# Griffin-style block with product-key experts on one core: the split of p is taken apart from its product, a gathered block's rows get a second buffer, a selection step ends at GpSimd's part

## The chip, the cores and the metric

One core of a Trainium2 chip runs the whole program. The engines are TensorE (PE, matmuls; PEld is its weight load), VectorE (DVE), ScalarE (ACT), GpSimd (POOL) and SyncE (SP, which here issues loads and stores). Each works through its own list of instructions in order, and semaphores tie the lists together. The metric is device time in microseconds (us), the median of several runs.

## What is computed

One layer of an encoder block for 1024 tokens of width 1024, in float32. Only the last part, the PEER feed-forward, is touched by the change:

```python
def peer_ffn(hn, w_query, sub_keys, expert_u, expert_v):   # per chunk xc of 128 tokens
    q = (xc @ w_query).reshape(c, PEER_HEADS, 2, PEER_HALF_DIM)
    sc = jnp.einsum('chpd,hpnd->chpn', q, sub_keys)          # scores of 2 x 128 keys, 8 heads
    s1, i1 = lax.top_k(sc[:, :, 0], 16)
    s2, i2 = lax.top_k(sc[:, :, 1], 16)
    cand = s1[..., :, None] + s2[..., None, :]               # 256 pairs
    top, pos = lax.top_k(cand.reshape(c, 8, 256), 16)        # 16 experts of 128*128, per head
    g = softmax(top)
    a = gelu(einsum('chkd,cd->chk', expert_u[eidx], xc))
    return einsum('chk,chkd->cd', g * a, expert_v[eidx])
...
h = h + peer_ffn(rmsnorm(h, ffn_norm_w), ...)
return rmsnorm(h, final_norm_w)
```

## The kernel before

The 1024 tokens are eight tiles of 128. First come the projections, attention, convolution, gates, and the query scores of all tiles; none of that is changed. After that the experts are computed, in two ways at once.

**Dense, for five tiles (640 tokens).** All 16384 experts are run over all 640 tokens, 128 experts at a time: 128 rounds, which this text calls expert blocks, numbered `i`. Operands are split into a high part (a rounded copy) and a low part (the difference), and each product takes three matmuls: high by high, high by low, low by high. One round does this:

- `expert_z`: PE multiplies the block's 128 rows of `expert_u` (tiles `uh`, `uhl`) with the tokens (`actTh`, `actTl`) into `z`, 48 matmuls of 320 columns. ACT takes the Gelu of `z` into `pr` (line 942).
- `expert_p`: DVE multiplies `pr` by the weights `wt` (line 946). Then `split` makes two tiles of it: ACT copies it, rounded, into `ph` (line 906), and DVE subtracts `ph` from `pr` into `phl` (line 908). So on DVE two instructions stand next to each other, and the second needs a result of ACT that needs the first.
- `expert_v`: the block's rows of `expert_v` are loaded and split in the same way (`vh` by ACT, `vhl` by DVE), and `expert_u(i + 1)` loads and splits the next round's `uh` and `uhl`.
- `expert_out`: PE multiplies `ph`, `phl` of two finished blocks with `vh`, `vhl`. There are ten pieces (five token tiles, two halves of 512 columns), five in an even round and five in an odd round. Four of the ten stay in PSUM for the whole loop (`held`). The other six are called moving: each goes to one of two PSUM buffers (`pout`), and DVE adds it to `hacc` in SBUF (line 975). A moving piece can start on PE only when DVE has added the piece two before it. The even round has the pieces moving, held, moving, held, moving; the odd round has held, moving, held, moving, moving. The callback `after` is called before the second piece of a round, and does the product and the split of p.

**Gathered, for three tiles (384 tokens), which the names call blocks `c`.** For each of 128 chosen experts per token, POOL issues an indirect load of 128 rows of 2048 floats (`uvt`, line 741, four buffers). DVE forms the dot product with the block's own rows `hng` (line 748), ACT makes the weight (lines 750 and 751), and DVE adds the weighted second half to `acc` (line 761). `hng` has one buffer and is loaded by SP at the start of each of the three blocks (line 737). These steps come from a generator, `gather_gen`.

**Selection of the three gathered tiles.** `select_gen` finds the experts of a tile in two halves, step by step: top 16 on DVE (`top16`), and at the end, for each of two index lists, a comparison on DVE (line 637), a multiplication on POOL (line 639) and a reduction of its result on DVE (line 640). All three stand in one step.

**What sets the order.** PE and DVE run in the order in which the code is written from the dense loop on; ACT, POOL and SP are ordered by the scheduler. The side jobs are interleaved by `tick`: each group of matmuls counts off its nominal time, and a generator's next step is written out whenever its period is used up. A gather step has a period of 2.36 us while the selection runs and 1.78 us after it; a selection step has 13 us (`SEL_STEP_D`). One round counts off 12.8 us.

Of the kernel before, what the change touches and what calls it, by code (L numbers as in the profile page):

```python
# [10 lines left out]
F32 = mybir.dt.float32  # L11
BF16 = mybir.dt.bfloat16
F32R = mybir.dt.float32r
# [7 lines left out]
P = 128  # L21
S = 1024
D = 1024
# [4 lines left out]
GB = NB * P  # L28
# [17 lines left out]
PHB = 4  # L46
# [6 lines left out]
WFB = 2  # L53
GATHER = (2.36, 1.78)
SEL_STEP = 1.5
SEL_STEP_D = 13
W_STEP = 1.6
MIXW = 3
ATT = (5, 4)
# [6 lines left out]
def block_kernel(ctx, tc, x, wqkv, wcols, wpr, wo, wq, skT, uv, uT, an_w, fn_w, fin_w, sub_w,  # L66
                 conv_w, lq1, lk1, lq2, lk2, cosT, sinT, out):
    nc = tc.nc
    V, A, PL, PE, SP = nc.vector, nc.scalar, nc.gpsimd, nc.tensor, nc.sync
# [524 lines left out]
    def select_gen(small, tt, ev, gw, done=None):  # L594
        hh = PH // 2
        sh = [P, hh, TOPK, TOPK]
        s3 = [P, hh, TOPK]

        t = small

        for a in range(2):
            sc = t([P, PH, NK], F32, "sc")
            SP.dma_start(out=sc, in_=sc_d[tt * P:(tt + 1) * P, a * PH * NK:(a + 1) * PH * NK]
                         .rearrange("p (h c) -> p h c", c=NK))
            sv, si = t([P, PH, TOPK], F32, "sv"), t([P, PH, TOPK], U32, "si")
            for hp in range(PH):
                top16(t, sc[:, hp, :], NK, sv[:, hp, :], si[:, hp, :])
                yield
            ohs = sc.rearrange("p h c -> p (h c)").bitcast(BF16).rearrange("p (j h a k) -> p j h a k", j=2, a=TOPK, k=TOPK)
            sf = t([P, PH, TOPK], F32, "sf")  # L610
            V.tensor_copy(out=sf, in_=si)
            svv = sv.rearrange("p (h q) k -> p h q k", q=2)
            sfv = sf.rearrange("p (h q) k -> p h q k", q=2)
            tv, ti = t(s3, F32, "tv"), t(s3, U32, "ti")
            cd = t([P, hh, CAND], F32, "cd")
            for c0, a0, na, nb in ((0, 0, 4, TOPK), (64, 4, TOPK - 4, 4)):
                sc2 = [P, hh, na, nb]
                V.tensor_tensor(out=cd[:, :, c0:c0 + na * nb].rearrange("p h (a b) -> p h a b", b=nb),
                                in0=svv[:, :, 0, a0:a0 + na].unsqueeze(3).broadcast_to(sc2),
                                in1=svv[:, :, 1, :nb].unsqueeze(2).broadcast_to(sc2), op=ALU.add)  # L620
            yield
            for h in range(hh):
                top16(t, cd[:, h, :], CAND, tv[:, h, :], ti[:, h, :])
                yield
            for j in range(2):
                pi, pj, pf = t(s3, U32, "pi"), t(s3, U32, "pj"), t(s3, BF16, "pf")
                if j == 0:
                    V.tensor_scalar(pi, ti, 4, None, op0=ALU.logical_shift_right)
                    V.tensor_scalar(pj, ti, 2, None, op0=ALU.logical_shift_right)
                    V.scalar_tensor_tensor(pf, pj, -12.0, pi, op0=ALU.add, op1=ALU.max)  # L630
                else:
                    V.tensor_scalar(pi, ti, 12, None, op0=ALU.bitwise_and)
                    V.tensor_scalar(pj, ti, 3, None, op0=ALU.bitwise_and)
                    V.scalar_tensor_tensor(pf, ti, 64.0, pi, op0=ALU.is_lt, op1=ALU.mult)
                    V.tensor_tensor(out=pf, in0=pf, in1=pj, op=ALU.add)
                oh = ohs[:, j]
                V.tensor_tensor(out=oh, in0=pf.unsqueeze(2).broadcast_to(sh), in1=iota_k.unsqueeze(1).broadcast_to(sh),
                                op=ALU.is_equal)
                PL.tensor_tensor(out=oh, in0=oh, in1=sfv[:, :, j, :].unsqueeze(3).broadcast_to(sh), op=ALU.mult)
                V.tensor_reduce(out=ev[j][:, a * 64:(a + 1) * 64].rearrange("p (h k) -> p h k", k=TOPK),  # L640
                                in_=oh.rearrange("p h a k -> p h k a"), axis=AX.X, op=ALU.add)
                yield
            dv = t(s3, F32, "dv")
            V.tensor_tensor(out=dv, in0=tv, in1=tv[:, :, 0:1].broadcast_to(s3), op=ALU.subtract)
            A.activation(tv, dv, AF.Exp)
            zz = t([P, hh], F32, "zz")
            V.tensor_reduce(out=zz, in_=tv, axis=AX.X, op=ALU.add)
            V.reciprocal(out=zz, in_=zz)
            V.tensor_tensor(out=gw[:, a * 64:(a + 1) * 64].rearrange("p (h k) -> p h k", k=TOPK), in0=tv,
                            in1=zz.unsqueeze(2).broadcast_to(s3), op=ALU.mult)  # L650
            if done:
                done(a * 64, (a + 1) * 64)
            yield
# [73 lines left out]
    def gather_gen(gat):  # L727
        st = {}

        def slot():  # L730
            return gat.tile([P, 2 * D], F32, name="uvt", tag="uvt", bufs=UVT)

        def fetch(c, k):
            if k == 0:
                st[c] = gat.tile([P, D], F32, name="hng", tag="hng")
                rows = slice(sels[c][0] * P, (sels[c][0] + 1) * P)
                SP.dma_start(out=st[c], in_=hn_d[rows, :])
                st["acc", c] = gat.tile([P, D], F32, name="acc", tag="acc")
                SP.dma_start(out=st["acc", c], in_=h_d[rows, :])
            t = slot()  # L740
            PL.indirect_dma_start(out=t[:], out_offset=None, in_=uv,  # L741
                                  in_offset=bass.IndirectOffsetOnAxis(ap=sels[c][1][:, k:k + 1], axis=0))
            return c, k, t

        def dot(c, k, t):
            u = t[:, 0:D]
            zt = tiny.tile([P, 1], F32, name="zt", tag="zt")
            V.scalar_tensor_tensor(u, u, 1.0, st[c], op0=ALU.mult, op1=ALU.mult, accum_out=zt)  # L748
            wt = tiny.tile([P, 1], F32, name="wt", tag="wt")
            A.activation(wt, zt, AF.Gelu)  # L750
            A.activation(wt, wt, AF.Copy, scale=sels[c][2][:, k:k + 1])
            return c, k, t, wt, fetch_last() if k == NE - 1 else None

        def fetch_last():
            t = slot()
            SP.dma_start(out=t[:, 0:D], in_=bass.AP(tensor=fin_w.tensor, offset=fin_w.offset, ap=[[0, P], [1, D]]))
            return t[:, 0:D], t[:, D:2 * D]

        def accumulate(c, k, t, wt, end):
            acc = st["acc", c]  # L760
            V.scalar_tensor_tensor(acc, t[:, D:2 * D], wt, acc, op0=ALU.mult, op1=ALU.add)  # L761
            yield
            if end:
                fw, y = end
                ss = tiny.tile([P, 1], F32, name="ss_o", tag="ss_o")
                A.activation(y, acc, AF.Square, accum_out=ss)
                if c < NA - 1:
                    yield
                r = rstd_of(ss, D, 1, "o")
                state["normed"] = c  # L770
                yield
                V.scalar_tensor_tensor(y, acc, r, fw, op0=ALU.mult, op1=ALU.mult)
                SP.dma_start(out=out[sels[c][0] * P:(sels[c][0] + 1) * P, :], in_=y)

        held = dotted = None
        for c in range(NA):
            while c >= len(sels):
                yield
            for k in range(NE):
                while k >= got[sels[c][0]]:  # L780
                    yield
                new = fetch(c, k)
                if held:
                    held = dot(*held)
                    yield
                    if dotted:
                        yield from accumulate(*dotted)
                    dotted = held
                held = new
        held = dot(*held)  # L790
        yield
        yield from accumulate(*dotted)
        yield from accumulate(*held)
# [99 lines left out]
    du, dn, dv, hp, gat = (pool(n) for n in ("du", "dn", "dv", "hp", "gat"))  # L893
# [51 lines left out]
    def expert_p(i, p):  # L945
        V.tensor_mul(p.rearrange("p (c t) -> p c t", t=WT), p.rearrange("p (c t) -> p c t", t=WT),
                     wts[i // WB][:, :, i % WB, :])
        return split(p, "ph", PHB, [P, GB], V)

    def expert_v(i):  # L950
        vr = raw_rows(uv[i * P:(i + 1) * P, D:])
# [10 lines left out]
    def expert_out(pv, vv, part, first, last, after):  # L962
        n = len(order) // BLK
        for j, (t, hf) in enumerate(order[part * n:(part + 1) * n]):
            if j == 1:
                after()
            ds = slice(hf * 512, (hf + 1) * 512)
            lhs = [(p[0][:, t * P:(t + 1) * P], p[1][:, t * P:(t + 1) * P]) for p in pv]
# [31 lines left out]
    for i in range(NK + BLK):  # L1000
        b, part = i // BLK - 1, i % BLK
        made = []
# [4 lines left out]
                us.append(expert_u(i + 1))  # L1007

        def product():
            if made:  # L1010
                pv.append(expert_p(i, made.pop()))

        if i < NK:
            made.append(expert_z(i, us.pop(0), ahead))
        if b >= 0:
            expert_out(pv[:BLK], vv[:BLK], part, b == 0, b == NK // BLK - 1, product)
        product()
        if b >= 0 and part == BLK - 1:
            pv, vv = pv[BLK:], vv[BLK:]
        if i < NK:  # L1020
# [70 lines left out]
```

## Time and profile before

| | |
|---|---|
| median of 3 runs | 3399.04 us (3398.12 to 3399.4) |
| profiled execution | 3390.54 us, its span 3388.8 us |
| busy share of the span | PE 91%, PEld 83%, DVE 78%, ACT 38%, POOL 26% |
| mean granted TensorE clock | 0.959 of full speed |
| dense loop in the span | from 1315 us to 3370 us |
| loaded and stored | 801 MB |

A busy share is an average over all stages. In the dense loop two engines are nearly full, so what each of them waits for, and where, says more than the shares. In rows of the trace a name to the left of the arrow is what an instruction writes, to the right what it reads, and the bracket at the end tells how long its engine had stood idle and what ended that.

### The profile page before, as it was taken

How to read it: one execution, taken by the hardware profiler on the slowest of the kernel's cores; microseconds unless marked ns; L12 is line 12 of the kernel's file. 1: busy time of each engine (PE TensorE's matmuls, PEld its weight loads, DVE VectorE, ACT ScalarE, POOL GpSimd, SP SyncE). 2: the span in 40 equal slices, each digit the busy share in tenths (PEclk: the TensorE clock that was granted, in tenths of full speed). 3: DMA queues.
4: the chain of work that ended last, by engine and by line, in shares of the span. 5: the costliest groups of instructions: out<-in, count | busy, mean ns of one | idle time of the engine just before them, and what ended most of it. 6: DMA issues, size and time to landing. Idle time of an engine off the chain costs nothing.

```text
span 3388.8 us, 45651 instructions
## 1 busy us (share of the span) xinstructions
PE 3073.1 (91%) x17551; PEld 2804.0 (83%) x17551; DVE 2659.0 (78%) x4661; ACT 1295.8 (38%) x2341; POOL 889.2 (26%) x712
## 2 busy tenths in 40 slices
PE   8999999898989887998998998998999988999896
PEld 6799988798988787887887887887888877888785
DVE  4442564589999965988898987888988888888888
ACT  3322462446577674323223323323223332333232
POOL 2310000154353542222222222222222322223232
PEclk9999999899999998999999998999999998999999
DMA  4442223735443656777787877787777888898886
GB/s 172 156 152 73 85 87 118 248 127 212 162 176 145 230 217 240 279 268 268 273 291 262 286 267 254 278 285 254 285 282 248 325 308 303 324 324 329 293 323 247
DMA packets 237547, 801.09 MB, mean 236 GB/s; under 512 B 18832, under 2 KB 123280, under 8 KB 174096
## 3 DMA queue, kind: packets, MB, share of 16 engines
q0 software_dynamic: 64704, 442.53, 35.3%
q1 hardware_dynamic: 152592, 305.30, 26.5%
q10 hardware_dynamic: 20032, 50.34, 3.9%
q8 instruction: 138, 2.26, 0.3%
q14 instruction: 81, 0.66, 0.1%
HBM read 714.74 MB, written 83.36 MB: 236 GB/s over the span
## 4 chain that ended last, share of the span: by engine, by line
PE 26%; issue 24%; DVE 22%; DMA 11%; POOL 9%; ACT 7%; SPq 0%; POOLq 0%; ACTq 0%; DVEq 0%
POOL uvt L741 8%; DMA raw<-in_uT 6%; PE pg L228 4%; DVE acc L761 3%; DVE uvt L748 3%; PE pq L228 3%; PE z L915 3%; PE ph L228 2%; DVE hacc L975 2%; PE py L228 2%; DVE vhl L908 2%; PE pout L915 2%; PE pw L694 2%; DVE phl L908 1%; DMA uvt<-in_uv,idx 1%
## 5 line engine op out<-in xcount | busy, mean ns | idle before, releaser
L741 POOL DMA_INDIRECT uvt<-in_uv,idx x384 | 498.4, 1298 | 1498.3 <-DVE acc L761 1447.3
L915 PE MATMUL z<-actTh,uhl 128*128 128x320 f32 x2048 | 645.1, 315 | 13.6 <-DVE uhl L908 13.6
L915 PE MATMUL z<-actTh,uh 128*128 128x320 f32 x2048 | 647.4, 316 | 7.7 <-ACT pr L942 5.8
L915 PE MATMUL z<-actTl,uh 128*128 128x320 f32 x2048 | 645.5, 315 | 0.0
L748 DVE SCALAR_TENSOR_TENSOR uvt<-uvt,hng 128x1024 f32<-128x1024 f32 x384 | 467.5, 1217 | 54.2 <-DMA uvt<-in_uv,idx 26.9
L761 DVE SCALAR_TENSOR_TENSOR acc<-uvt,wt,acc 128x1024 f32<-128x1024 f32 x384 | 490.7, 1278 | 5.3 <-DMA acc<-h_d 5.0
L915 PE MATMUL pout<-vh,ph 128*128 128x512 f32 x768 | 319.0, 415 | 175.9 <-DVE hacc L975 175.8
L915 PEld LDWEIGHTS z<-actTh,uh 128*128 128x128 f32 x2048 | 398.4, 195 | 15.4 <-ACT pr L942 6.7
L915 PEld LDWEIGHTS z<-actTh,uhl 128*128 128x128 f32 x2048 | 396.8, 194 | 14.0 <-DVE uhl L908 14.0
L915 PEld LDWEIGHTS z<-actTl,uh 128*128 128x128 f32 x2048 | 397.6, 194 | 6.6
L750 ACT ACTIVATE wt<-zt 128x1 f32<-128x1 f32 x384 | 77.0, 201 | 721.3 <-DVE uvt L748 721.0
L915 PEld LDWEIGHTS pout<-vh,ph 128*128 128x128 f32 x768 | 149.0, 194 | 231.8 <-DVE hacc L975 204.5
L915 PE MATMUL pout<-vhl,ph 128*128 128x512 f32 x768 | 311.7, 406 | 1.6 <-DVE vhl L908 1.6
L915 PE MATMUL pout<-vh,phl 128*128 128x512 f32 x768 | 311.6, 406 | 0.0
L975 DVE TENSOR_TENSOR hacc<-pout,hacc 128x512 f32<-128x512 f32 x384 | 262.2, 685 | 28.9 <-PE pout L915 27.9
L717 POOL TENSOR_TENSOR o<-ms,wtr 128x512 f32<-128x512 bf16 x160 | 204.5, 1322 | 255.0 <-PE pw L694 132.4
L185 DVE TENSOR_TENSOR wl<-wr,wh 128x2048 fp32r<-128x2048 f32 x66 | 157.9, 2393 | 113.9 <-ACT wh L184 113.9
L906 ACT CAST uh<-raw 128x1024 fp32r<-128x1024 f32 x128 | 134.7, 1052 | 280.1 <-DMA raw<-in_uT 226.0
L908 DVE TENSOR_TENSOR phl<-pr,ph 128x640 fp32r<-128x640 f32 x128 | 105.6, 825 | 152.6 <-ACT ph L906 151.0
L694 PE MATMUL pw<-o,o 128*128 128x128 f32 x1280 | 172.4, 288 | 39.5 <-POOL o L717 19.1
L184 ACT CAST wh<-wr 128x2048 fp32r<-128x2048 f32 x74 | 141.0, 1907 | 164.4 <-DMA wr<-in_wq 33.2
L694 PEld LDWEIGHTS pw<-o,o 128*128 128x128 f32 x1280 | 164.2, 202 | 47.6 <-POOL o L717 24.0
(290 smaller groups left out, 6831.2 us busy)
## 6 DMA issues: line engine op xcount, KB each, us to landing
raw<-in_uT SPq DMA_DIRECT2D x128, 512.0 KB
raw<-in_uv SPq DMA_DIRECT2D x128, 512.0 KB
w_d<-wbuf ACTq DMA_DIRECT2D x20, 2048.0 KB
wt<-w_d SPq DMA_DIRECT2D x32, 1280.0 KB
wr<-in_wcols SPq DMA_DIRECT2D x28, 1024.0 KB
wr<-in_wq SPq DMA_DIRECT2D x24, 1024.0 KB
xt<-in_x SPq DMA_DIRECT2D x16, 512.0 KB
q_d<-qt POOLq DMA_DIRECT2D x32, 256.0 KB
```

What stands on the lines that cost most here:

```text
L184: A.copy(out=op[0][sl], in_=src)
L185: lo.tensor_sub(op[1][sl], src, op[0][sl].bitcast(F32))
L228: PE.matmul(pd, lhsT=l[a], rhs=r[b], start=i == 0 and j == 0, stop=i == n - 1 and j == len(c) - 1)
L694: PE.matmul(pw[:, u, :], lhsT=o2[:, t + u, :], rhs=o1[:, t + u, :], start=True, stop=True)
L717: PL.tensor_tensor(out=o1.rearrange("p t i -> p i t"), in0=ms[:, 0], in1=w[:, ts].unsqueeze(1).broadcast_to(sh), op=ALU.mult)
L741: PL.indirect_dma_start(out=t[:], out_offset=None, in_=uv, in_offset=bass.IndirectOffsetOnAxis(ap=sels[c][1][:, k:k + 1], axis=0))
L748: V.scalar_tensor_tensor(u, u, 1.0, st[c], op0=ALU.mult, op1=ALU.mult, accum_out=zt)
L761: V.scalar_tensor_tensor(acc, t[:, D:2 * D], wt, acc, op0=ALU.mult, op1=ALU.add)
L906: A.copy(out=hi, in_=t)
L908: eng.tensor_sub(lo, t, hi.bitcast(F32))
L915: PE.matmul(ps, lhsT=lhs[k][a], rhs=rhs[k][b], start=first and k == 0 and j == 0, stop=last and k == n - 1 and j == 2)
L975: V.tensor_add(hacc[:, t - NR, ds], ps, hacc[:, t - NR, ds])
```

## The change

There are three edits, all of which act in the dense loop.

1. The split of p. `expert_p` now does the product on DVE and the copy on ACT, and leaves out the subtraction. That is a function of its own, `expert_lo`, which is called at the next call of `after`; and `after` is called before the second and before the fourth piece of a round.
2. `hng` has two buffers.
3. A selection step of a gathered tile ends after POOL's multiplication, so the reduction stands in the following step. Each half then has 18 steps for 16, and the period goes from 13 to 11.6 us: 208.8 us for a half, after 208.

```diff
-SEL_STEP_D = 13
+SEL_STEP_D = 11.6
...
                 PL.tensor_tensor(out=oh, in0=oh, in1=sfv[:, :, j, :].unsqueeze(3).broadcast_to(sh), op=ALU.mult)
+                if done:
+                    yield
                 V.tensor_reduce(out=ev[j][:, a * 64:(a + 1) * 64].rearrange("p (h k) -> p h k", k=TOPK),
...
-                st[c] = gat.tile([P, D], F32, name="hng", tag="hng")
+                st[c] = gat.tile([P, D], F32, name="hng", tag="hng", bufs=2)
...
-        return split(p, "ph", PHB, [P, GB], V)
+        hi = dv.tile([P, GB], F32R, name="ph", tag="ph", bufs=PHB)
+        A.copy(out=hi, in_=p)
+        return p, hi
+
+    def expert_lo(p, hi):
+        lo = dv.tile([P, GB], F32R, name="phl", tag="phl", bufs=PHB)
+        V.tensor_sub(lo, p, hi.bitcast(F32))
+        return hi, lo
...
-            if j == 1:
+            if j in (1, 3):
                 after()
...
         def product():
-            if made:
-                pv.append(expert_p(i, made.pop()))
+            if made and isinstance(made[0], tuple):
+                pv.append(expert_lo(*made.pop()))
+            elif made:
+                made[0] = expert_p(i, made[0])
...
-        product()
+        while made:
+            product()
```

The order of instructions on PE is the same as before, and so are all lists ahead of the dense loop. Three places show what moves. The first is DVE in an odd round of the dense loop: `pr<-pr,wt` is the product, `phl<-pr,ph` the subtraction, `hacc` the three moving pieces, and `uvt,zt` and `acc` are gather steps. Before:

```order
L946 TENSOR_TENSOR pr<-pr,wt 128x640
L908 TENSOR_TENSOR phl<-pr,ph 128x640
L975 TENSOR_TENSOR hacc<-pout,hacc 128x512
L761 SCALAR_TENSOR_TENSOR acc<-uvt,wt,acc 128x1024
L975 TENSOR_TENSOR hacc<-pout,hacc 128x512
```

Now, in such a round:

```order
L948 TENSOR_TENSOR pr<-pr,wt 128x640
L984 TENSOR_TENSOR hacc<-pout,hacc 128x512
L763 SCALAR_TENSOR_TENSOR acc<-uvt,wt,acc 128x1024
L956 TENSOR_TENSOR phl<-pr,ph 128x640
L642 TENSOR_REDUCE e_18983<-sc 128x64
L984 TENSOR_TENSOR hacc<-pout,hacc 128x512
```

One moving piece's addition and one gather step now stand between the product and the subtraction; the reduction of the selection happens to follow here.

The second place is DVE at a selection step of a gathered tile: `sc<-pf,iota_k` is the comparison, and the reduction writes `e`. Before:

```order
L637 TENSOR_TENSOR sc<-pf,iota_k 128x1024
L640 TENSOR_REDUCE e_18969<-sc 128x64
L975 TENSOR_TENSOR hacc<-pout,hacc 128x512
L908 TENSOR_TENSOR vhl<-raw,vh 128x1024
L748 SCALAR_TENSOR_TENSOR uvt,zt<-uvt,hng 128x1024
```

Now:

```order
L637 TENSOR_TENSOR sc<-pf,iota_k 128x1024
L763 SCALAR_TENSOR_TENSOR acc<-uvt,wt,acc 128x1024
L984 TENSOR_TENSOR hacc<-pout,hacc 128x512
L956 TENSOR_TENSOR phl<-pr,ph 128x640
L750 SCALAR_TENSOR_TENSOR uvt,zt<-uvt,hng 128x1024
L984 TENSOR_TENSOR hacc<-pout,hacc 128x512
L910 TENSOR_TENSOR vhl<-raw,vh 128x1024
L763 SCALAR_TENSOR_TENSOR acc<-uvt,wt,acc 128x1024
L910 TENSOR_TENSOR uhl<-raw,uh 128x1024
L750 SCALAR_TENSOR_TENSOR uvt,zt<-uvt,hng 128x1024
L642 TENSOR_REDUCE e_18983<-sc 128x64
```

The reduction stands ten instructions later, and what follows the comparison at once is an addition of the gather, whose operands both lie in SBUF.

The third place is SP's queue at the start of the dense loop. Before, the loads of the first gathered block are followed by the dense loop's:

```order
L737 DMA hng<-hn_d 128x1024
L739 DMA acc<-h_d 128x1024
L934 DMA wt<-w_d 128x20x128
L923 DMA raw<-in_uv 128x1024
L923 DMA raw<-in_uT 128x1024
```

Now:

```order
L739 DMA hng<-hn_d 128x1024
L741 DMA acc<-h_d 128x1024
L936 DMA wt<-w_d 128x20x128
L739 DMA hng<-hn_d 128x1024
L925 DMA raw<-in_uv 128x1024
L925 DMA raw<-in_uT 128x1024
```

The second block's `hng` is loaded here, ahead of two of the dense loop's loads, and no longer at that block's start.

## Rows read from the trace of the kernel before

**Rows 1.** Windows: start:end length, busy per engine, clock, DMA share, GB/s

```profile
1315.00:1366.00 51.00, 33.29 (x175) 31.19 (x176) 21.41 (x33) 14.17 (x24) 8.24 (x7) 0.77 0.88 313
1366.00:2624.00 1258.00, 1158.02 (x6244) 1041.80 (x6243) 1092.13 (x1781) 383.56 (x769) 298.93 (x228) 0.96 0.77 272
2624.00:3336.00 712.00, 637.26 (x3430) 573.43 (x3429) 616.59 (x777) 219.66 (x489) 205.02 (x156) 0.96 0.87 315
```

**Rows 2.** Waits of PE, 1315 to 3370: sum in us, times, longest

```profile
PE pout L915 <- DVE hacc L975: 175.8, 65, 12.1
```

**Rows 3.** Waits of DVE, 1366 to 2624

```profile
DVE phl L908 <- ACT ph L906: 85.3, 79, 3.3
DVE e L640 <- POOL sc L639: 20.7, 10, 2.1
DVE hacc L975 <- PE pout L915: 20.4, 23, 2.7
DVE pr L946 <- ACT pr L942: 17.0, 10, 5.5
```

**Rows 4.** Waits of DVE, 2624 to 3336

```profile
DVE phl L908 <- ACT ph L906: 61.5, 44, 8.2
DVE uvt L748 <- DMA uvt<-in_uv,idx: 19.8, 25, 2.0
DVE hacc L975 <- PE pout L915: 4.8, 5, 2.0
```

**Rows 5.** PE in order of time, 2637 to 2652: start, duration, instruction

```profile
2637.57 0.31 PE L915 MATMUL z<-actTh,uh 128*128 128x320 f32 x1
...
2651.49 0.31 PE L915 MATMUL z<-actTh,uh 128*128 128x320 f32 x1
```

**Rows 6.** PE in order of time around a wait, 2663 to 2669

```profile
2663.82 0.39 PE L915 MATMUL pout<-vh,phl 128*128 128x512 f32 x1
2667.73 0.73 PE L915 MATMUL pout<-vh,ph 128*128 128x512 f32 x1 [3.52 <-DVE hacc L975]
2668.26 0.63 PE L915 MATMUL pout<-vhl,ph 128*128 128x512 f32 x1
```

**Rows 7.** Windows, right behind that wait

```profile
2667.70:2670.30 2.60, 2.57 (x6) 2.11 (x7) 2.60 (x3) 0.95 (x1) 0.95 (x1) 0.53 0.45 186
```

**Rows 8.** DVE in order of time, 1407 to 1412

```profile
1407.49 0.82 DVE L946 TENSOR_TENSOR pr<-pr,wt 128x640 f32<-128x640 f32 x1
1409.11 0.83 DVE L908 TENSOR_TENSOR phl<-pr,ph 128x640 fp32r<-128x640 f32 x1 [0.80 <-ACT ph L906]
1409.85 1.28 DVE L761 SCALAR_TENSOR_TENSOR acc<-uvt,wt,acc 128x1024 f32<-128x1024 f32 x1
1411.05 0.68 DVE L975 TENSOR_TENSOR hacc<-pout,hacc 128x512 f32<-128x512 f32 x1
```

**Rows 9.** ACT in order of time, same place

```profile
1406.84 1.06 ACT L906 CAST uh<-raw 128x1024 fp32r<-128x1024 f32 x1
...
1408.35 0.73 ACT L906 CAST ph<-pr 128x640 fp32r<-128x640 f32 x1
```

**Rows 10.** Waits of DVE, 1315 to 3370

```profile
DVE phl L908 <- ACT ph L906: 151.0, 126, 8.2
DVE uvt L748 <- DMA hng<-hn_d: 26.8, 2, 25.1
```

**Rows 11.** POOL in order of time, 1079.7 to 1081.9

```profile
1079.76 1.94 POOL L639 TENSOR_TENSOR sc<-sc,sf 128x1024 bf16<-128x1024 bf16 x1 [3.64 <-DVE rz L395]
```

**Rows 12.** DVE in order of time, 1079.7 to 1081.9

```profile
1079.59 0.16 DVE L395 RECIPROCAL rz<-zs 128x2 f32<-128x2 f32 x1
1079.79 1.92 DVE L396 SCALAR_TENSOR_TENSOR rz<-rz,nlam,zs 128x1 f32<-128x1 f32 x1
```

**Rows 13.** POOL in order of time, 3067.0 to 3067.3

```profile
3067.26 1.68 POOL L741 DMA_INDIRECT uvt<-in_uv,idx  x1 [2.99 <-DVE acc L761]
```

**Rows 14.** DVE in order of time, 3076.8 to 3077.1

```profile
3077.00 1.23 DVE L748 SCALAR_TENSOR_TENSOR uvt<-uvt,hng 128x1024 f32<-128x1024 f32 x1 [1.23 <-DMA uvt<-in_uv,idx]
```

## The prediction

> **What bounds the kernel now.** The edits act only in the dense loop, so I began with the windows by stage, and took its two long parts: 1258 us with the selection beside the gather (80 rounds) and 712 us without it (44 rounds) [rows 1]. In both, DVE is busy for 87% and PE for 89 to 92%, so the next question is which of them waits for the other. PE's waits have one large row: 175.8 us, 65 times, for DVE's addition to `hacc` [rows 2]; that is one round in two, the odd one, whose last two pieces are both moving. DVE's waits for PE are small: 20.4 and 17.0 us in the first part (the second of these through ACT's Gelu), 4.8 us in the other [rows 3, 4]. So DVE sets the pace, and PE stands when DVE is behind. DVE's largest loss is not work but a wait for ACT: the subtraction `phl` behind the copy `ph`, 85.3 and 61.5 us [rows 3, 4], 151.0 us over the loop [rows 10].
>
> How much could be won at all is read from PE in an undisturbed round: from the first `z` matmul of one to that of the next 13.92 us [rows 5]. The two parts take 1258 / 80 = 15.72 and 712 / 44 = 16.18 us a round. At 13.92 us they would be shorter by 144 and 100 us. A wait of PE costs more than its length: behind one of 3.52 us the granted clock was 0.53 for 2.60 us, the lower of the two levels for nearly all of it, which is about 1.2 us more [rows 6, 7].
>
> **The split of p.** The number of instructions is unchanged: 128 products, copies and subtractions. What changes is what stands between product and subtraction. In the timeline of DVE the product starts at 1407.49 and takes 0.82; ACT's copy runs from 1408.35 for 0.73, and the subtraction starts at 1409.11, after 0.80 us of standing [rows 8, 9]. Now an addition of a moving piece (0.68) and mostly a gather step (1.28 for `acc`) stand there [rows 8], 1.9 us or so, which covers 0.80. That is 0.80 x 126 = 101 us of the 151.0. The other 50 us belong to copies that come late, up to 8.2 us [rows 10]: on ACT the cast `uh` of the next expert block, which waits for a load, stands ahead of `ph` [rows 9], and the new list of ACT still has it there. The cover exceeds 0.80 by about 1.1 us, so of each late copy up to 1.1 us more is hidden; I take 30 of the 50. Together -131 us of DVE time; bounds -101 (no late copy gains) and -151. In the odd round the subtraction moreover stands behind the first addition to `hacc`, which PE is waiting for; that comes 0.80 + 0.74 us earlier.
>
> No new wait is queued behind: the copy needs only gather steps that stand before the product on DVE, as it did. What is held longer is `pr`, which has one buffer; the subtraction is done some 2 us later, while the next Gelu comes only when PE has gone through the next `z`, some half of a round later, so that is at no cost.
>
> **The selection step.** It removes DVE's wait for POOL's multiplication, 20.7 us, 10 times [rows 3]. But the wait has a second cause that stays. Earlier in the program the multiplication ran for 1.94 us from 1079.76, and a DVE instruction of one column, started 0.03 us later, took 1.92 us and ended with it, where its neighbour of two columns took 0.16 [rows 11, 12]. So a DVE instruction that meets the multiplication can be held to its end. In the new order seven of the ten comparisons are followed by a gather step, with both operands in SBUF, the other three by an addition from PSUM and only then by such an instruction. I take -3 us, bounds 0 and -20.7.
>
> The Trainium skill ("SBUF — State Buffer", section "SBUF: two separate sides") says that VectorE, with two SBUF inputs, and GpSimd share a port pair that one of them holds for a whole instruction while the other is blocked. The trace agrees with 1.92 us beside 1.94. By that rule the edit is worth about nothing; without it, 20.7 us.
>
> The two steps more for a half at 11.6 us leave its end where it was (208.8 for 208 us). At 11.6 us against the 12.8 us that a round counts off, a round gets two steps now and then; the top 16 of a step is eight short instructions, and their sum is unchanged.
>
> **The second buffer.** DVE waited for `hng` twice, 26.8 us, of which 25.1 once [rows 10]. That one is the first block's load, which no buffer shortens. What can go is 1.7 us. Against it, 512 KB more are loaded in the 51 us at the loop's start, ahead of two loads of the dense loop; at the 313 GB/s of that stretch [rows 1] this is 1.7 us. I take 0, bounds -2 and +2.
>
> **What comes back.** With 131 us less for DVE, rounds approach 13.92 us, and DVE will meet PE more often. Its waits for PE are 42 us now. They could double (+42); but many of them follow rounds in which PE ran at the lower clock, and these get fewer (-20). I take +5. The gather's loads are the other thing: in the second part the DMA engines are busy for 0.87 at 315 GB/s [rows 1], DVE waits 19.8 us for `uvt` [rows 4], and one load took from 3067.26 to 3077.00, 9.7 us [rows 13, 14]. If a round there shrinks by 7%, DVE offers each of the four buffers that much less. I take +8, bounds 0 and +62, the whole gain of that part.
>
> **The sum.** -131 - 3 + 0 + 5 + 8 = -121 us, against the profiled execution's 3390.54 us. The median of the runs is 3399.04, 8.5 us more; I carry the difference over: 3278 us. About 80 us of it should show in the first part and 40 in the second.
>
> **Rivals.**
>
> *PE's floor is reached.* The earlier addition to `hacc` removes most of PE's waits, their lower clock goes with them, and a round comes to 14.3 us in the first part and 14.6 in the second: 80 x 1.42 + 44 x 1.58 = 183 us, 3216 us. For it: DVE without its waits needs about as much as PE (1258 us less the 143 us of the four waits in [rows 3], 13.9 us a round). Against: the 12.8 us that a round counts off hold 5.4 gather steps at 2.36 us and 7.2 at 1.78, so that one round has more of them than the next, and both engines can hardly be full at once when only two PSUM buffers lie between them.
>
> *The gather's loads take it.* In the second part DVE's waits for `uvt` grow by what the split releases: -121 + 50 = -71 us, 3328 us. For it: the 0.87 and the 9.7 us. Against: in 2667.70 to 2670.30 the core moves 186 GB/s [rows 7], so it is not steadily full, and no wait for these loads was longer than 2.0 us [rows 4].
>
> *The subtraction waits all the same.* If ACT's copy comes later than DVE's two instructions in most rounds, because the new list puts other things ahead of it, only the long stands shrink: some -35 us, 3364 us. Against: in the rows the copy starts as soon as the product is out, 0.04 us after.
>
> *Slower: the even rounds begin to wait.* The subtraction now stands ahead of the second-last addition of the odd round and the last of the even one. Where the copy is late, PE's moving pieces of both rounds hang on it. If each of the 64 even rounds took a wait like the odd rounds', 175.8 / 65 = 2.7 us [rows 2], and 1.2 us for the clock [rows 7], that is 64 x 3.9 = +250 us against -121: 3528 us. It decides from half of them on: from 31 even rounds the change is slower. Against: before, the subtraction stood ahead of these additions as well, and of one more.
>
> **Chances.** The forecast (3232 to 3310) 0.66; PE's floor 0.12; the gather's loads 0.13; the subtraction waits all the same 0.05; slower 0.04. The range 3232 to 3338 takes in the forecast, most of the third case and little of the second. A measurement of this kernel tells some 0.2%, 7 us, from no change. All cases but the last lie beyond that on the faster side; of the fourth I give 0.02 to no change. Faster 0.94, same 0.02, slower 0.04.
>
> **What would show it.** Right: DVE's row `phl` waiting for `ph` falls from 151 us to 20 or so, with longest ones left; PE's row for `hacc` falls by more than half, and rounds beside it lose the stretches of low clock; the reduction's wait for POOL is gone, and instructions of 1.2 us next to the multiplication show up with some 1.9 us more. `uvt`'s wait stays under 40 us. Wrong: a row of DVE for `uvt` or for `pout` over 60 us, a `phl` row over 60 us, or PE waiting for `hacc` in even rounds.

## The result, and the profile after

The changed kernel takes 3278.13 us in the median of its runs (3268.35 to 3290.3), before 3399.22; the ratio is 0.9646, with a 95% interval of 0.9611 to 0.9681. A second set of runs gave 0.9657 (0.9633 to 0.9681). The forecast was 3278. One run of one kernel below, the one with the callback before the third piece, took 6942.12 us where its other three took 3320, and is left out of that kernel's time. The profiled execution shown here took 3282.6 us, its span 3280.8. From profile to profile the gain is 108 us and not 121: the profile of before lies 8.5 us under its median, this one 4.5 us over its own.

The dense loop went from 2054 us to 1949, from 1312.6 to 3261.7 in the new span. First the windows of its two long parts, to be read against [rows 1] (start:end, length, busy time of PE, PEld, DVE, ACT and POOL, clock, DMA share, GB/s):

```profile
1364.00:2538.00 1174.00, 1132.09 (x6245) 1028.12 (x6244) 1096.48 (x1778) 381.81 (x770) 307.66 (x227) 0.99 0.82 292
2538.00:3229.00 691.00, 634.15 (x3433) 570.43 (x3433) 615.65 (x780) 222.81 (x490) 205.13 (x157) 0.97 0.89 324
```

The first part is 84 us shorter and the second 21. In the first a round now takes 14.7 us, near PE's 13.92 [rows 5], and the granted clock rose from 0.96 to 0.99. In the second the DMA engines went from 315 to 324 GB/s and a round still takes 15.7 us, after 16.2.

Next PE's waits in the loop, against [rows 2] (sum in us, times, longest):

```profile
PE pout L917 <- DVE hacc L984: 101.5, 44, 7.3
```

That was 175.8 us, 65 times. And DVE's waits in the loop, against [rows 3, 4, 10]:

```profile
DVE uvt L750 <- DMA uvt<-in_uv,idx: 60.4, 48, 4.5
DVE phl L956 <- ACT ph L951: 51.5, 17, 8.0
DVE uvt L750 <- DMA hng<-hn_d: 25.0, 1, 25.0
DVE hacc L984 <- PE pout L917: 15.8, 26, 2.0
DVE zz L649 <- ACT tv L647: 12.8, 5, 4.5
DVE pr L948 <- ACT pr L944: 5.0, 6, 1.5
```

The wait for the copy of p fell from 151.0 us, 126 times, to 51.5 us, 17 times: the short ones are gone, the long ones are not. The wait for the gather's loads more than doubled, from 26.9 us. Most of that lies in the second part, where these two rows stand against 61.5 and 19.8 us in [rows 4]:

```profile
DVE uvt L750 <- DMA uvt<-in_uv,idx: 49.7, 39, 4.5
DVE phl L956 <- ACT ph L951: 14.9, 5, 4.2
```

What a long wait for the copy of p looks like is seen on ACT, in order of time:

```profile
1861.23 1.05 ACT L908 CAST uh<-raw 128x1024 fp32r<-128x1024 f32 x1 [10.40 <-DMA raw<-in_uT]
...
1862.62 0.71 ACT L951 CAST ph<-pr 128x640 fp32r<-128x640 f32 x1
```

and on DVE at the same place:

```profile
1863.36 0.82 DVE L956 TENSOR_TENSOR phl<-pr,ph 128x640 fp32r<-128x640 f32 x1 [8.05 <-ACT ph L951]
```

ACT stood 10.40 us for a load of `expert_u`, with the copy of p behind it in its list, and DVE stood 8.05 us for the copy.

At a selection step, the wait for POOL is gone from the rows, and this stands in its place on DVE:

```profile
1751.45 0.69 DVE L637 TENSOR_TENSOR sc<-pf,iota_k 128x1024 bf16<-128x1024 bf16 x1
1752.06 1.28 DVE L763 SCALAR_TENSOR_TENSOR acc<-uvt,wt,acc 128x1024 f32<-128x1024 f32 x1
1753.26 0.68 DVE L984 TENSOR_TENSOR hacc<-pout,hacc 128x512 f32<-128x512 f32 x1
1753.86 2.36 DVE L910 TENSOR_TENSOR vhl<-raw,vh 128x1024 fp32r<-128x1024 f32 x1
```

with POOL beside it:

```profile
1752.28 2.86 POOL L639 TENSOR_TENSOR sc<-sc,sf 128x1024 bf16<-128x1024 bf16 x1 [3.59 <-issue]
```

The subtraction `vhl`, 1.2 us elsewhere, took 2.36 and ended 1.1 us after POOL did. The ten multiplications of the loop have one such instruction each, 1.1 to 1.7 us too long, 14 us in all.

### The profile page after: what moved, and what is told of

Same layout as the page of the kernel before. It is cut to its first block, busy times and chain, and to the rows that moved or that the text cites. A ratio compares the mean times of both kernels' runs of the same rounds, so it can differ in the third digit from the quotient of the medians.

```text
span 3280.8 us, 45680 instructions
## 1 busy us (share of the span) xinstructions
PE 3038.2 (93%) x17551; PEld 2781.1 (85%) x17551; DVE 2665.3 (81%) x4661; ACT 1296.1 (40%) x2341; POOL 900.4 (27%) x712
## 4 chain that ended last, share of the span: by engine, by line
PE 33%; DVE 24%; issue 20%; DMA 10%; POOL 7%; ACT 5%; SPq 1%; POOLq 0%; ACTq 0%; DVEq 0%
POOL uvt L743 7%; PE z L917 6%; PE pg L228 4%; DVE acc L763 4%; DMA raw<-in_uT 4%; DVE uvt L750 4%; PE pout L917 4%; PE pq L228 3%; PE ph L228 2%; DVE hacc L984 2%; PE held L917 2%; DVE vhl L910 2%; PE py L228 2%; DMA uvt<-in_uv,idx 2%; PE pw L696 2%
## 5 line engine op out<-in xcount | busy, mean ns | idle before, releaser
L750 DVE SCALAR_TENSOR_TENSOR uvt<-uvt,hng 128x1024 f32<-128x1024 f32 x384 | 471.8, 1229 | 85.6 <-DMA uvt<-in_uv,idx 60.4
L917 PE MATMUL pout<-vh,ph 128*128 128x512 f32 x768 | 311.2, 405 | 101.7 <-DVE hacc L984 101.5
L917 PE MATMUL pout<-vh,phl 128*128 128x512 f32 x768 | 305.0, 397 | 0.0
L984 DVE TENSOR_TENSOR hacc<-pout,hacc 128x512 f32<-128x512 f32 x384 | 261.1, 683 | 17.6 <-PE pout L917 15.8
L908 ACT CAST uh<-raw 128x1024 fp32r<-128x1024 f32 x128 | 134.7, 1052 | 270.5 <-DMA raw<-in_uT 219.6
L917 PE MATMUL held<-vh,ph 128*128 128x512 f32 x512 | 199.9, 390 | 0.0
## 6 DMA issues: line engine op xcount, KB each, us to landing
wt<-w_d SPq DMA_DIRECT2D x32, 1280.0 KB, 14.7
```

Source lines behind the costliest of these rows:

```text
L908: A.copy(out=hi, in_=t)
L917: PE.matmul(ps, lhsT=lhs[k][a], rhs=rhs[k][b], start=first and k == 0 and j == 0, stop=last and k == n - 1 and j == 2)
L984: V.tensor_add(hacc[:, t - NR, ds], ps, hacc[:, t - NR, ds])
```

## The experiments

Times are medians; a ratio is against runs of the kernel before on the same chip.

**Each edit by itself.** The first edit alone leaves out these lines of the change:

```diff
-SEL_STEP_D = 11.6
+SEL_STEP_D = 13
...
-                if done:
-                    yield
...
-                st[c] = gat.tile([P, D], F32, name="hng", tag="hng", bufs=2)
+                st[c] = gat.tile([P, D], F32, name="hng", tag="hng")
```

> The kernel before with the first edit alone (the split of p). Theory A (the whole gain is the split; the other two edits give back what they take): 3278 us, within 10; DVE's wait of phl for ph at some 50 us as in the changed kernel, the reduction's wait for POOL still about 20 us. Theory B (the edits share the gain, some 20 us from the selection step and a few from the second buffer): 3300 us.

Measured: 3291.24 us, ratio 0.9676 (0.9647 to 0.9706). That is 110 of the 121 us, between the two theories.

The third edit alone, on the kernel before:

```diff
-SEL_STEP_D = 13
+SEL_STEP_D = 11.6
...
+                if done:
+                    yield
```

> The kernel before with the third edit alone (the selection step ends at POOL's multiplication). Theory A (a DVE instruction beside the multiplication is held to its end): within 6 us of before, 3393 to 3405; the wait of 20.7 us is gone, and some 14 us come back as ten stretched DVE instructions, about 8 as a longer wait of the softmax sum for ACT. Theory B (the wait is simply gone): 3378 to 3385.

Measured: 3405.6 us, ratio 1.0012 (0.9993 to 1.0031). Nothing, as theory A has it; DVE's wait `zz` is 13.8 us there, after 4.9. Its DVE, in order of time at one of the steps:

```profile
1539.52 0.68 DVE L977 TENSOR_TENSOR hacc<-pout,hacc 128x512 f32<-128x512 f32 x1
1540.12 2.58 DVE L763 SCALAR_TENSOR_TENSOR acc<-uvt,wt,acc 128x1024 f32<-128x1024 f32 x1
```

and POOL:

```profile
1539.69 1.93 POOL L639 TENSOR_TENSOR sc<-sc,sf 128x1024 bf16<-128x1024 bf16 x1 [3.83 <-DVE sc L637]
```

The addition from PSUM ran beside the multiplication in its usual 0.68 us; the gather's addition, with both operands in SBUF, took 2.58 for 1.28.

The second edit alone:

```diff
-                st[c] = gat.tile([P, D], F32, name="hng", tag="hng")
+                st[c] = gat.tile([P, D], F32, name="hng", tag="hng", bufs=2)
```

> The kernel before with the second edit alone (two buffers for hng). Theory A: within 4 us of before, since only 1.7 us of the waits for hng can go. Theory B (the ends of the gathered blocks are long because the next block's rows come late): 10 us or more faster, the rounds 49 and 93, of 27.5 and 27.1 us, shorter by 5 each.

Measured: 3404.26 us, ratio 1.0015 (0.9997 to 1.0032). Theory A. The wait of 24.5 us at the loop's start stays, as in the changed kernel. The round 49 is as long as before (27.3 us, PE waits 12 us in it), so the late rows were not what makes it long; the round 93 takes 24.0 us after 27.1, but the time of the whole did not follow.

**The first two edits without the third.**

```diff
-SEL_STEP_D = 11.6
+SEL_STEP_D = 13
...
-                if done:
-                    yield
```

> The changed kernel without its third edit (split of p and second buffer). Theory A: the same as the changed kernel, 3270 to 3290. Theory B (with DVE relieved, the selection's wait counts): 3295 to 3300.

Measured: 3292.27 us, 0.969 (0.9657 to 0.9722), nearer to theory B. So I ran the whole change again, with more rounds:

> The changed kernel again, unaltered, beside the kernels of this call and to be set against the split alone (ratio 0.9676) and the split with the second buffer (0.969). Theory A (the other two edits give nothing on top of the split): ratio 0.967 to 0.969. Theory B (with DVE relieved by the split, the selection step counts, some 13 us): 0.963 to 0.966.

Measured: 3276.81 us, 0.9657 (0.9633 to 0.9681): on theory B's side by its middle, but the intervals overlap. It took a kernel with less spread to decide this (below).

**What holds the second part.** The gather with half the bytes. This kernel fetches only one half of a row, and of other rows than the layer asks for, so what it computes is not the layer; it serves for its time alone.

```diff
-            PL.indirect_dma_start(out=t[:], out_offset=None, in_=uv,
+            PL.indirect_dma_start(out=t[:, 0:D], out_offset=None, in_=uv.rearrange("n (a d) -> (n a) d", a=2),
...
-            V.scalar_tensor_tensor(acc, t[:, D:2 * D], wt, acc, op0=ALU.mult, op1=ALU.add)
+            V.scalar_tensor_tensor(acc, t[:, 0:D], wt, acc, op0=ALU.mult, op1=ALU.add)
```

> The changed kernel, but a gather load fetches rows of 1024 floats instead of 2048 (every second row of the table's halves, read by the same index), and the addition to acc uses the same half as the dot product: half the bytes, every instruction of DVE, ACT and PE kept. Theory A (in the second part the gather's loads bind): the wait for uvt falls from 60 us to under 10, the second part from 691 us to 650, the run to 3235. Theory B (the coupling of PE and DVE binds, and DVE would wait for something else): 3268 or more.

Measured: 3182.47 us, 0.9355 (0.9337 to 0.9374). The second part in its windows:

```profile
2503.00:3130.00 627.00, 617.10 (x3433) 560.71 (x3432) 613.27 (x780) 222.15 (x491) 215.87 (x157) 1.00 0.69 228
```

and PE's row:

```profile
PE pout L917 <- DVE hacc L984: 27.1, 22, 4.6
```

Theory A, and more than it said. A round takes 14.25 us there, the wait for `uvt` fell to 4.5 us over the loop, and the wait for the copies of p to 3.4 us: their loads were late beside the gather's. With the same instructions on DVE and PE, PE is 98% busy in this part, and the first part is shorter too, 1136 us after 1173. So both kinds of wait that the change leaves are waits for loads.

**The late copies.** Four buffers for `raw`; the room comes from `hng`:

```diff
-                st[c] = gat.tile([P, D], F32, name="hng", tag="hng", bufs=2)
+                st[c] = gat.tile([P, D], F32, name="hng", tag="hng")
...
-        t = du.tile([P, D], F32, name="raw", tag="raw", bufs=3)
+        t = du.tile([P, D], F32, name="raw", tag="raw", bufs=4)
...
-        fin_b = rows_bcast(du, fin_w, D, "fin_d", "raw", 3)
+        fin_b = rows_bcast(du, fin_w, D, "fin_d", "raw", 4)
```

> The changed kernel with four buffers for raw (the loads of expert_u and expert_v) instead of three, and one for hng, which makes room for it. Theory A (the copies of p that come late stand behind a cast uh whose load was issued late, because its buffer came free late): DVE's wait of phl for ph falls from 51 us to under 20, the run to 3250 to 3265. Theory B (the loads are late because the DMA engines are full, in the second part above all): earlier issue gains nothing, the gather's waits grow by as much; 3270 to 3285.

Measured: 3242.22 us, 0.9534 (0.9519 to 0.955), some 35 us under the changed kernel on the same chip (3276.81), better than theory A's range. DVE's row, and two of ACT's:

```profile
DVE phl L956 <- ACT ph L951: 3.4, 2, 2.6
```

```profile
ACT uh L908 <- DMA raw<-in_uT: 16.6, 4, 8.0
ACT uh L908 <- PE z L917: 306.4, 100, 7.8
```

In the changed kernel they are these:

```profile
ACT uh L908 <- DMA raw<-in_uT: 219.6, 90, 10.4
ACT uh L908 <- PE z L917: 50.5, 10, 6.6
```

The same bytes through the same queues, but issued one buffer earlier: ACT hardly stands for them. It stands for PE instead, which still reads the `uh` that the cast is to overwrite; that wait ends in step with PE, and the copy of p behind the cast is in time. Theory B falls. DVE waits 33.0 us for `hng`, after 25.0, since that has one buffer here, so the fourth `raw` buffer won this back too. The same on the kernel before:

```diff
-        t = du.tile([P, D], F32, name="raw", tag="raw", bufs=3)
+        t = du.tile([P, D], F32, name="raw", tag="raw", bufs=4)
...
-        fin_b = rows_bcast(du, fin_w, D, "fin_d", "raw", 3)
+        fin_b = rows_bcast(du, fin_w, D, "fin_d", "raw", 4)
```

> The kernel before with four raw buffers instead of three, and no other edit. Theory A (of the 151 us of waits of phl for ph, some 50 belong to copies that stand behind a late cast uh): the wait falls to 102 us, 0.80 for each of 128, and the run to 3350 to 3365. Theory B (the late copies matter only when rounds are short): 3390 to 3400, PE's waits for hacc about as long as before.

Measured: 3327.22 us, 0.9788 (0.9759 to 0.9818).

```profile
DVE phl L908 <- ACT ph L906: 104.8, 128, 4.0
```

The wait fell as theory A said, to 0.82 us for each of 128. The time fell by 73 us, below theory A's range and some 27 more than the wait. The Gelu, which stands on the same engine, is in time too: DVE's wait for it went from 21.0 us to 6.3, and its wait for PE's pieces from 27.9 to 19.9. So this one number, by itself, gives more than half of what the three edits give.

**The place of the subtraction.**

```diff
-            if j in (1, 3):
+            if j in (1, 2):
                 after()
```

> The changed kernel with the callback before the second and the third piece of a round, instead of the second and the fourth, so that the subtraction stands one piece earlier: in an even round only a gather step or nothing is between product and subtraction, in an odd round one addition. Theory A (the cover between the two is what counts): the wait of phl for ph rises from 51 to 75 to 110 us, the run to 3295 to 3320. Theory B (that PE's piece is added before the subtraction counts, which the odd round keeps): 3270 to 3288.

Measured: 3320.1 us, 0.9768 (0.9732 to 0.9804).

```profile
DVE phl L956 <- ACT ph L951: 99.9, 60, 7.2
```

Theory A, at the edge of its range: some 42 us of the gain hang on what stands between product and subtraction. The wait rose by 48 us against the changed kernel.

**The selection step again, where PE hardly waits.** The kernel with four raw buffers, without the third edit (the same lines as above):

```diff
-SEL_STEP_D = 11.6
+SEL_STEP_D = 13
...
-                if done:
-                    yield
```

> The kernel with four raw buffers and one for hng (raw4), without the third edit, so that the selection step ends at the reduction as before. PE hardly waits there, and its times spread little. Theory A (the selection step gives back what it takes, about nothing): within 5 us of raw4's 3242. Theory B (with DVE relieved it counts): 3252 to 3262.

Measured: 3258.92 us, 0.9579 (0.9555 to 0.9603), against 0.9534 (0.9519 to 0.955) with the edit: 17 us, and the intervals are apart. Theory B. PE's row with the edit:

```profile
PE pout L917 <- DVE hacc L984: 69.8, 37, 10.2
```

and without it:

```profile
PE pout L915 <- DVE hacc L982: 91.5, 36, 12.6
```

Without it, a step looks like this on DVE, with a wait of 2.05 us for POOL's multiplication between the two:

```profile
1552.14 0.69 DVE L637 TENSOR_TENSOR sc<-pf,iota_k 128x1024 bf16<-128x1024 bf16 x1
1554.88 2.15 DVE L640 TENSOR_REDUCE e<-sc 128x64 f32<-128x1024 bf16 x1 [2.05 <-POOL sc L639]
```

The rounds of the first part in which a comparison or a reduction stands on DVE are over 13.92 us by 16 us in all with the edit (18 rounds) and by 38 without it (11 rounds); all other rounds there differ by 3 us, the other way. The same sum is 14 us in the profile of the changed kernel, 21 in that of its second set of runs and 36 with the first two edits, but 54 with the third edit alone and 50 before. So the gain lies in the rounds that the edit touches, and is there only with the split. The other rounds vary by as much from profile to profile: in the two of the changed kernel they are 4 and 20 us longer than with the first two edits. That the period went from 13 to 11.6 us along with it, in every run, is not taken apart from the place of the step's end.

**The pace of the gather.**

```diff
-GATHER = (2.36, 1.78)
+GATHER = (2.2, 1.95)
```

> The changed kernel with gather periods 2.2 and 1.95 us instead of 2.36 and 1.78: more of the gather beside the selection, less in the second part. Theory A (the first part now has room, the second is held by loads): second part 25 us shorter, first part some 10 longer, 3260 to 3268. Theory B (DVE is full in both): what the second part gains the first one loses, 3273 to 3290.

Measured: 3274.36 us, 0.964 (0.9616 to 0.9664), the same as the changed kernel. The first part takes 1204 us and the second 645, that is +30 and -46 against the changed kernel's profile and +39 and -44 against its second one: theory B, nearly. With four raw buffers, and half of the shift:

```diff
-GATHER = (2.36, 1.78)
+GATHER = (2.28, 1.86)
```

> raw4 with gather periods 2.28 and 1.86 us instead of 2.36 and 1.78, half the shift of the run with 2.2 and 1.95. Theory A (the first part has room now that the late copies are gone, the second is held by the gather's loads): second part 20 us shorter, first part 8 longer, 3230. Theory B (each microsecond moved costs as much in the first part): 3237 to 3247.

Measured: 3227.29 us, 0.949 (0.9464 to 0.9516), the fastest of all, 15 us under `raw4`'s median; the interval is just apart from that kernel's. Its two parts:

```profile
1370.00:2518.00 1148.00, 1122.30 (x6241) 1019.43 (x6240) 1107.81 (x1801) 388.29 (x784) 319.61 (x236) 1.00 0.84 305
2518.00:3176.00 658.00, 628.53 (x3437) 566.87 (x3436) 599.00 (x759) 217.57 (x476) 196.34 (x151) 0.98 0.90 330
```

against 1142 and 682 us of the kernel without the shift: theory A. Half of the shift cost 6 us in the first part here, the whole of it 30 or more in the changed kernel, so room seems to be there once the late copies are gone; the two shifts differ in size, so this is not shown by itself.

## Why the prediction came out, term by term

The time was met, and the mechanism was the one named: DVE sets the pace of the dense loop, its wait for ACT's copy was the largest loss, and something useful stands between product and subtraction now. The terms under it were less exact than their sum.

- **The split of p: -131 forecast, about -100 measured on its row** (151.0 to 51.5 us, 42.5 in the profile of the second set of runs). The short waits went as reckoned. The step that failed is that 30 of the 50 us of late copies would be hidden by a longer cover. On the rows of before it comes out: 1.1 us off each of the waits above 0.80 leaves 20 of the 50. But it took the copies to be as late as before, and they are later now. Taken from the end of DVE's product to the start of ACT's copy, and added up where it is over 0.2 us, the delay was 52 us in 40 rounds before and is 102 us in 46 rounds; delays of more than 1.15 us, which the cover of 1.9 us can't hide, went from 14 to 29. In some rounds more than 1.9 us stands there, so 17 waits of 3 us on average are left. This was the lower bound, -101. It is the loads: the delay is 11 us with the gather's bytes halved, and 2 us, in one round, with four buffers for `raw`. Why the loads fall further behind is not shown by a run of its own; that rounds are shorter, with as many buffers as before, would do it.
- **The selection step: -3 forecast.** The mechanism was seen rightly in [rows 11, 12]: a DVE instruction is held by POOL's multiplication, 14 of the 20.7 us come back that way, 8 more as a longer wait of `zz` (4.9 to 12.8 us), and alone the edit gives nothing. What the forecast missed is that the same DVE time, spread over two rounds, is worth more than in one piece when PE is close behind. Comparison, wait and reduction were 0.6 + 2.05 + 2.1 us in a row, and PE's moving pieces need DVE's additions meanwhile. With the split that costs PE's waits: the edit was worth 14 to 15 us there by the medians of the changed kernel and of the first two edits, whose intervals overlap, and 17 in the kernel with four raw buffers, where they are apart.
- **The second buffer: 0 forecast, nothing measured** (1.0015 alone; on top of the split 3292.27 after 3291.24).
- **DVE's waits for PE: +5 forecast, -28 measured** (27.9 + 21.0 us to 15.8 + 5.0). The text had a fall as a bound, because many of these waits follow rounds at the lower clock. The clock of the first part did rise from 0.96 to 0.99, but that this is the cause is not shown: 16 of the 28 us are DVE's wait for ACT's Gelu, and a fourth buffer for `raw` alone, on the kernel before, took 15 us off that wait.
- **The gather's loads: +8 forecast, +33 measured** (26.9 to 60.4 us). The rival that named them was right in its place and over half in its price: in the second part their wait grew by 30 us, and that part gained 21 us, not 40. With half-sized loads it took 627 us, 15 above PE's floor of 44 x 13.92. By the text's own mark (over 60 us) this term was wrong.

On the rows the sum is -100 for the split, about +1 for the selection step, -2 for `hng`, -28 for PE and +33 for the gather: -96 us, and the loop became shorter by 105. DVE's whole account closes that: it stands idle for 187.1 us of the loop, after 295.7, and is busy for 1762.7, after 1759.4, which is -109 and +3. So the 14 us of held instructions make only 3 us of busy time. Some 6 us of the difference are overlap: an instruction that follows without a wait starts about 0.08 us before the one ahead has ended, as at 1752.06 in the rows above, and fewer waits leave more of that. The rest is open.

So the total was met because a term mis-sized by 31 us and one by 25 were mostly balanced by one mis-sized by 33 and by this overlap. In the two profiles the gain is 13 us short of the forecast. That the forecast hit the median to the microsecond is chance; that it lay within 20 us is not.

Of the signs that the text gave, three failed besides the row for `uvt`. `phl` was to fall to 20 us or so and stands at 51.5. PE's row for `hacc` was to fall by more than half and fell by 42%. And PE does wait in even rounds, 8 times and 10.9 us in all after 3 times and 2.4 us, 9.7 us of it in the second part.

Of the other rivals: PE's floor was nearly reached only where loads were taken out of the way (3182 us with half the bytes). The subtraction did not wait all the same. The even rounds did not begin to wait in the first part (one wait of 0.8 us), where 55 of 80 rounds are now within 0.3 us of PE's floor, after 26.

## What to carry to other kernels

- Where one engine's list has producer and consumer next to each other with another engine between them, two instructions of other work in between are worth the whole round trip (0.8 us here; of 126 waits 17 are left). They hide the ordinary latency; they don't hide a consumer that is late because a load is late. For that, look at what stands ahead of it on the middle engine, and issue that load one buffer earlier.
- A wait that is replaced by a held instruction gives nothing as engine time. It can still be worth something if it breaks up a long piece of one engine's work that another engine's small buffer can't bridge, and here this showed only once the other engine was nearer to its floor: the value of the edit alone (0 us) and on top of another (14 to 17 us) differ.
- When two engines are relieved at once, ask what they then pull faster: in the second part, where the DMA engines were busy for 0.87, DVE's wait for the gather's loads took back 30 of the 47 us that the split released there. And a delay that was measured in the old, slower loop can grow in the new one.

## What was not expected of the hardware

- Beside POOL's multiplication of two SBUF operands, DVE's addition of a PSUM and an SBUF operand ran at its usual 0.68 us, while the next instruction with two SBUF operands took 2.58 us for 1.28. The other way round, a DVE instruction of this kind that was already running kept POOL waiting: 2.86 us for the multiplication, 1.93 otherwise. That bears out the Trainium skill ("SBUF — State Buffer", section "SBUF: two separate sides"), which has whichever of the two starts first keep the shared ports for a whole instruction, where the DVE instruction has two SBUF inputs. The addition of a PSUM and an SBUF operand has only one, and none of those that ran beside a multiplication in these traces took more than 0.69 us.
- One more buffer for loads that were already on their way three deep took ACT's standing for them from 219.6 to 16.6 us, at a DMA share of 0.83 after 0.82 in the first part. The loads had been issued too late for the time that they take beside the gather's; there was room for the same bytes earlier.
